# Expert products of a one-core decoder layer: only w3's second half stays an unsplit float32 product, and the down weights' parts move up in program order

## The chip, the cores and the metric

The kernel runs on one core of a Trainium2 chip. The metric is the device time of one execution in microseconds (us), median of the runs taken. The engines are named as the profile names them: PE (TensorE, the matmuls), PEld (its weight loads), ACT (ScalarE), DVE (VectorE), POOL (GpSimd) and SP (SyncE, which issues most transfers). Each engine runs its own instructions in order; they wait for one another on semaphores.

## The reference, cut to what matters

One layer of a decoder: stick-breaking attention and a state-space branch in parallel, then a mixture of experts with a final norm. The part that the change touches:

```python
def expert_block(args):
    xi, e = args                                   # 128 routed tokens, one of 32 experts
    hdn = jax.nn.silu(xi @ w1[e]) * (xi @ w3[e])   # 1024 -> 512
    return hdn @ w2[e]                             # 512 -> 1024
yb = lax.map(expert_block, (xb, block_e)).reshape(cap, d)
y = jax.ops.segment_sum(yb * slot_w[:, None], slot_tok, num_segments=t + 1)[:t]
```

All arrays are float32. There are 1024 tokens, 32 experts, and two experts for each token.

## The kernel before, in words

The program goes through the layer in stages; the experts are the last long one, the function `moe`. It loops over the 32 experts, one block of 128 token slots each. For expert e:

- `gather` (L1066) fetches the token rows by an indirect transfer, three experts ahead, into one of three row buffers.
- `xt` transposes the 128x1024 tokens on PE in two groups of four (L1088, into the PSUM tile `tr`). Tokens 0 to 511 of the model dimension are split: ACT copies them to float32r (`xh`), DVE subtracts that from the original (`xl`). The other half is copied by ACT as plain float32 (`xf`, L1090).
- The weights come as pages of 1 MB (128x2048 float32): w1 and w3 in two halves each, w2 in two halves, so six pages for each expert. SP loads them (L1052) into a ring of 14 page buffers named `r`, `m` and `x`, and waits for a buffer before each load.
- `unit` splits a page into two float32r tiles, the rounded part by ACT (L101) and the rest by DVE (L102). The two tiles are a pair; there are room and names for three pairs, `w` twice and `ms` once, given out in the order in which the program asks for units. A pair is taken over when the matmuls on its old unit are done.
- `up` multiplies. The first halves of w1 and w3 are units, with three matmuls for each 128 rows: high x high, high x low, low x high (L1112 to L1114). The second halves are unsplit float32 products with `xf` straight from the page (L1120). Both accumulate in the PSUM tiles `a1` and `a3`. Then ACT takes the sigmoid (L1126) and DVE multiplies twice (L1128), into the tile `mid`.
- `ht` transposes `mid` on PE (L1133) and splits the result into `hh` and `hl` (they are tile `w1_8641` in the rows below).
- `down` multiplies by the two units of w2, three matmuls for each 128x512 piece (L1145 to L1147), into `o0` and `o1`. ACT scales them into a row buffer (L1152) and POOL scatters it to DRAM (L1159).

In the loop, the down products of an expert run one expert late: the program order is `up(e)` first half, `ht` of e-1, `up(e)` second half, `xt(e+1)`, `down(e-1)`. The two w2 units are asked for inside `down`. A scheduler then sets the order of each engine's instructions; the tiles and their buffers keep the program's order. Each expert thus asks for four units: w1's and w3's first halves, then w2's two halves.

Of the kernel before, what the change touches and what calls it, by code (L numbers as in the profile page):

```python
# [12 lines left out]
F32 = mybir.dt.float32  # L13
F32R = mybir.dt.float32r
# [13 lines left out]
KD = D // 128  # L28
# [5 lines left out]
NE = 32  # L34
FF = 512
# [17 lines left out]
def _f(ap):  # L53
    return ap.bitcast(F32)
# [12 lines left out]
def drain(*gens):  # L67
    for g in gens:
        for _ in g:
            pass  # L70
# [924 lines left out]
def moe(tc, ctx, pool, i, ident, rt, ye_d, tab_d, h2_d, hg_d, split, con, out, rp, mp, wop, wop1, scale):  # L995
    nc = tc.nc
    V, A, P = nc.vector, nc.scalar, nc.gpsimd
    tab = rt["tab"]
    IO = bass.IndirectOffsetOnAxis
    XG, YB, NX, LAG = 3, 4, 2, 3  # L1000
# [5 lines left out]
    with ExitStack() as c:  # L1006
        ps = pool(c, "psb", space=PSUM)
        p = pool(c, "ex", bufs=2)

        rowr = [wop1.tile([128, 2, 512], F32R, name="w1", bufs=8) for _ in range(8)]  # L1010
        row = [_f(x).rearrange("p a b -> p (a b)") for x in rowr]
        hh, hl = (rowr[7][:, n].rearrange("p (a b) -> p a b", a=4) for n in range(2))
        xg, ss = row[:XG], p.tile([128, FF], F32, name="mid", bufs=1)
        ys = lambda e: row[XG + (e - NE + LAST) % YB]
        for x in xg:
            P.memset(x, 0.0)
# [4 lines left out]
        num = {}  # L1021
# [13 lines left out]
        raws, units = {}, {}  # L1035


        def view(t, shape):
            return t.rearrange("p a b -> p (a b)").rearrange("p (a b) -> p a b", a=shape[1])
# [5 lines left out]
        def ring(n, shape, r=False):  # L1045
            k = n if n < INIT else (n - INIT) % RING
            return page(*((rp, "r", 6) if k < 6 else (mp, "m", MR) if k < 12 else (p, "x", NX)), shape, r)

        def load(n):
            if n < len(src) and n not in raws:  # L1050
                raws[n] = ring(n, src[n][1])
                nc.sync.dma_start(raws[n], src[n][0])  # L1052

        def unit(n):

            if n not in units:
                load(n)
                pl, nm, b = (mp, "ms", 2) if len(units) % 3 == 2 else (wop, "w", 4)
                h, l = units[n] = [view(pl.tile([128, 4, FF], F32R, name=nm, bufs=b), src[n][1]) for _ in range(2)]
                split(h, l, raws[n], leng=P if n < HELD else V)  # L1060
            return units[n]

        def gather(e):
            if e >= NE - LAST:
                P.memset(xg[e % XG], 0.0)
            q = P.indirect_dma_start(out=xg[e % XG], out_offset=None, in_=hg_d, in_offset=IO(ap=tab[:, e, 0:1] if e else rt["idx"], axis=0),  # L1066
                                     bounds_check=S - 1, oob_is_err=False)
            first.append(q.ins)
# [11 lines left out]
        def xt(e):  # L1080

            x = xg[e % XG]
            xh, xl = (p.tile([128, 4, 128], F32R, name=n, bufs=1) for n in ("xh", "xl"))
            xf = p.tile([128, 4, 128], F32, name="xf", bufs=1)
            for q in range(2):
                tp = ps.tile([128, 4, 128], F32, name="tr", bufs=2)
                for k in range(4):
                    nc.tensor.transpose(tp[:, k], x[:, (q * 4 + k) * 128:(q * 4 + k) * 128 + 128], ident)  # L1088
                if q:
                    A.copy(xf, tp)  # L1090
                else:
                    parts[:] = split(xh, xl, tp)
            return xh, xl, xf

        gather(0)
        parts = []
        X = {0: xt(0)}
        read = rt["finish"](first[0], parts[1])
        with tc.issue_after(read):
# [6 lines left out]

        def up(e, xh, xl, xf):
            a = [ps.tile([128, 512], F32, name=n, bufs=2) for n in ("a1", "a3")]
            for w in range(2):
                h, l = unit(num[e, 0, w])  # L1110
                for k in range(4):
                    nc.tensor.matmul(a[w], lhsT=xh[:, k], rhs=h[:, k], start=(k == 0), stop=False)  # L1112
                    nc.tensor.matmul(a[w], lhsT=xh[:, k], rhs=l[:, k], start=False, stop=False)  # L1113
                    nc.tensor.matmul(a[w], lhsT=xl[:, k], rhs=h[:, k], start=False, stop=False)  # L1114
            yield
            for w in range(2):
                n = num[e, 1, w]
                load(n)
                for k in range(4):
                    nc.tensor.matmul(a[w], lhsT=xf[:, k], rhs=raws[n][:, k], start=False, stop=(k == 3))  # L1120
            yield

            s = ss.rearrange("p (k q) -> p k q", k=4)
            a = [x.rearrange("p (q k) -> p k q", k=4) for x in a]
            r = _f(tab[:, e, 3:4])
            A.activation(s, a[0], AF.Sigmoid, scale=r)  # L1126
            for n in range(2):
                V.scalar_tensor_tensor(s, a[n], r, s, op0=OP.mult, op1=OP.mult)  # L1128

        def ht():  # L1130
            tp = ps.tile([128, 4, 128], F32, name="tr", bufs=2)
            for k in range(4):
                nc.tensor.transpose(tp[:, k], ss[:, k * 128:k * 128 + 128], ident)  # L1133
            rooted[:] = split(hh, hl, tp)

        def down(e):
            o = [ps.tile([128, 512], F32, name=f"o{n}", bufs=1) for n in range(2)]
            for u in range(2):
                with tc.issue_after(rooted[0]) if e == NE - 1 and u else ExitStack():
                    h, l = unit(num[e, u, 2])  # L1140
                for n in range(2):
                    cs = slice(n * 512, n * 512 + 512)
                    for k in range(2):
                        kk = u * 2 + k
                        nc.tensor.matmul(o[n], lhsT=hh[:, kk], rhs=h[:, k, cs], start=(kk == 0), stop=False)  # L1145
                        nc.tensor.matmul(o[n], lhsT=hh[:, kk], rhs=l[:, k, cs], start=False, stop=False)  # L1146
                        q = nc.tensor.matmul(o[n], lhsT=hl[:, kk], rhs=h[:, k, cs], start=False, stop=(kk == 3))  # L1147
            done[:] = [q.ins]
            gate = _f(tab[:, e, 2:3])
            y = ys(e)  # L1150
            for n in range(2):
                A.activation(y[:, n * 512:n * 512 + 512], o[n], AF.Copy, scale=gate)  # L1152
            if e >= NE - LAST:
                yh, yl = last[e] = [wop1.tile([128, 2, 512], F32R, name="w1", bufs=8).rearrange("p a b -> p (a b)") for _ in range(2)]
                return lambda: split(yh, yl, y)
            scatter(e, y)
# [8 lines left out]
        def ahead(e):  # L1165
            for n in range(num[e, 0, 0], len(src)):
                load(n)

        def places():

            at = ring(len(src), [128, 2, D])
            P.iota(at[:, 0], pattern=[[1, S]], base=0, channel_multiplier=0, allow_small_or_imprecise_dtypes=True)
            hot = ring(len(src) + 1, [128, 2, S], True)
            for n in range(LAST):
                V.tensor_scalar(hot[:, n], at[:, 0], rt["tk"][:, NE - LAST + n:NE - LAST + n + 1], None, op0=OP.is_equal)
            g = at[:, 1]
            nc.sync.dma_start(g[:1], i["norm_final_g"].rearrange("(a d) -> a d", a=1))
            return hot, at

        def tiles(n, d, base):  # L1180

            b = []
            for t in range(0, NT, 2):
                b.append(ring(n + t // 2, [128, 2, D]))
                for k in range(2):
                    r = base + (t + k) * 128
                    nc.sync.dma_start(b[-1][:, k], d[r:r + 128, :])
            return b
# [7 lines left out]
        for e in range(NE):  # L1196
            g = up(e, *X[e])
            next(g)
            if e:
                ht()  # L1200
            if e == NE - 1:
                ahead(e)
                hot, at = places()
                res = tiles(len(src) + 2, h2_d, 0)
            drain(g)
            if e + XG < NE:
                gather(e + XG)
            if e + 1 < NE:
                X[e + 1] = xt(e + 1)
            if e:  # L1210
                parted = down(e - 1)
            if e == 1:
                zero = ys(3)
                P.memset(zero, 0.0)
                with tc.issue_after(first[-1]):
                    for n in range(NE - LAST, NE):
                        scatter(n, zero)
        overflow(at)
        ht()
        parted()  # L1220

        bs = []
        for t in range(0, NT, 2):
            n = len(src) + 6 + t
# [25 lines left out]
        for t in range(NT):  # L1250
            h, h1 = (x[:, t % 2] for x in bs[t // 2])
# [13 lines left out]
            ss, a, r, m = (p.tile([128, 1], F32, name=n) for n in ("ss", "ra", "rr", "rm"))  # L1265
# [136 lines left out]
```

## Time and profile before

| what | value |
|---|---|
| median of 3 runs | 1538.57 us (1536.74 to 1539.53) |
| the profiled execution | 1539.6 us, of which the span from first to last instruction is 1537.7 us |
| mean granted TensorE clock | 0.974 of full speed |
| PE busy | 1456.8 us, 95% of the span |
| DVE, ACT, POOL busy | 963.0, 722.3, 518.9 us |
| the expert stage | first token transposes at 864 us, last down product at 1493 us |

The profile is of one execution; its times are counted from the first instruction. Busy time is the time in which an instruction of the engine was running. A wait is the idle time of an engine before an instruction, put down to the instruction that released it.

### The profile page before, as it was taken

The page shows a single profiled execution, that of the slowest core. Times are in us where ns is not written, and L with a number is a line of the kernel's source. Part 1 is how long each engine was busy: PE and PEld are TensorE (multiplying, and loading weights), DVE is VectorE, ACT ScalarE, POOL GpSimd, SP SyncE. Part 2 cuts the span into 40 slices and gives each one's busy share as a digit, 9 for nine tenths or more (in the row PEclk, how much of TensorE's full clock was granted, in tenths as well). Part 3 has the DMA queues.
Part 4 walks back from the last instruction along what each step waited for, and adds up shares of the span by engine and source line. Part 5 has one row for each costly group of instructions (what it writes and reads, how often), then busy time and mean ns, then how long its engine had stood idle before and what let it go on. Part 6 is the DMA issues. An engine that isn't in the chain of part 4 may idle for free. (4 is left out here: it accounts for less than half of the span.)

```text
span 1537.7 us, 19509 instructions
## 1 busy us (share of the span) xinstructions
PE 1456.8 (95%) x6900; PEld 1123.4 (73%) x6900; DVE 963.0 (63%) x1488; ACT 722.3 (47%) x1141; POOL 518.9 (34%) x542
## 2 busy tenths in 40 slices
PE   7989799999999989999998799999999999999986
PEld 6967688998888867778787566666666666666663
DVE  6757565465756568665578566666665566656547
ACT  6212122455656577432223255555555455555543
POOL 1199941144444465332255321111111111111034
PEclk8999899999999999999999799999999999999998
DMA  8242344211111015264763799999999989999754
GB/s 256 77 104 72 92 104 97 60 42 54 30 51 34 28 44 142 78 198 160 268 247 124 286 346 356 352 354 353 356 360 351 353 342 358 334 334 357 271 200 163
DMA packets 132197, 314.77 MB, mean 205 GB/s; under 512 B 24305, under 2 KB 82289, under 8 KB 107522
## 3 DMA queue, kind: packets, MB, share of 16 engines
q1 hardware_dynamic: 120898, 295.99, 55.0%
q0 software_dynamic: 9728, 16.83, 2.9%
q8 instruction: 55, 0.90, 0.2%
q10 hardware_dynamic: 1472, 0.69, 0.2%
q14 instruction: 44, 0.36, 0.1%
HBM read 284.03 MB, written 44.11 MB: 213 GB/s over the span
## 5 line engine op out<-in xcount | busy, mean ns | idle before, releaser
L134 PE MATMUL mm<-xh,wh 128*128 128x512 f32 (+4 forms) x608 | 224.1, 369 | 1.1 <-DVE kl L691 0.6
L135 PE MATMUL mm<-xl,wh 128*128 128x512 f32 (+4 forms) x608 | 222.6, 366 | 0.0
L136 PE MATMUL mm<-xh,wl 128*128 128x512 f32 (+4 forms) x608 | 221.3, 364 | 0.8 <-DVE wl L102 0.8
L1159 POOL DMA_INDIRECT ye_d<-w,tab x32 | 56.1, 1754 | 250.0 <-ACT w L1152 249.4
L134 PEld LDWEIGHTS mm<-xh,wh 128*128 128x128 f32 x608 | 115.4, 190 | 16.0 <-issue 1.1
L136 PEld LDWEIGHTS mm<-xh,wl 128*128 128x128 f32 x608 | 115.4, 190 | 14.9 <-DVE wl L102 1.5
L135 PEld LDWEIGHTS mm<-xl,wh 128*128 128x128 f32 x608 | 115.3, 190 | 13.9 <-DVE xl L225 0.4
L754 DVE TENSOR_TENSOR_SCAN pr<-pr 128x144 f32<-128x144 f32 (+3 forms) x64 | 92.6, 1448 | 46.8 <-POOL pr L751 46.1
L102 DVE TENSOR_TENSOR w<-m,w 128x2048 fp32r<-128x2048 f32 x38 | 88.9, 2342 | 40.8 <-ACT w L101 40.7
L102 DVE TENSOR_TENSOR w<-r,w 128x2048 fp32r<-128x2048 f32 x36 | 82.2, 2291 | 47.6 <-ACT w L101 47.2
L1066 POOL DMA_INDIRECT w<-hg_d,tab x31 | 34.8, 1122 | 222.0 <-PE tr L1088 217.1
L755 POOL TENSOR_TENSOR be<-be,pr 128x143 f32<-128x143 f32 (+3 forms) x64 | 89.4, 1400 | 38.4 <-DVE pr L754 36.0
L1120 PE MATMUL a<-r,xf 128*128 128x512 f32 x224 | 100.7, 592 | 0.0
L1120 PE MATMUL a<-m,xf 128*128 128x512 f32 x208 | 93.3, 592 | 0.0
L1128 DVE SCALAR_TENSOR_TENSOR mid<-a,tab,mid 128x512 f32<-128x512 f32 x64 | 47.9, 749 | 63.8 <-ACT mid L1126 52.0
L101 ACT CAST w<-r 128x2048 fp32r<-128x2048 f32 x38 | 72.1, 1903 | 27.5 <-PE a L1113 14.4
L101 ACT CAST w<-m 128x2048 fp32r<-128x2048 f32 x38 | 72.5, 1907 | 18.9 <-PE o L1146 10.3
L101 ACT CAST wh<-wr 128x1024 fp32r<-128x1024 f32 (+1 forms) x44 | 44.6, 1014 | 65.8 <-PE mm L135 57.3
L1120 PEld LDWEIGHTS a<-r,xf 128*128 128x128 f32 x224 | 41.8, 190 | 42.3 <-issue 40.4
L102 DVE TENSOR_TENSOR wl<-wr,wh 128x1024 fp32r<-128x1024 f32 (+1 forms) x44 | 57.1, 1297 | 23.6 <-ACT wh L101 23.5
L1146 PE MATMUL o<-w,w 128*128 128x512 f32 x172 | 68.6, 399 | 3.2 <-DVE w L102 3.2
L751 POOL TENSOR_SCALAR_AFFINE_SELECT pr<-pr 128x128 f32<-128x128 f32 x64 | 26.3, 411 | 132.9 <-ACT pr L748 113.1
(534 smaller groups left out, 3766.2 us busy)
## 6 DMA issues: line engine op xcount, KB each, us to landing
r<-in_w_dram SPq DMA_DIRECT2D x84, 1024.0 KB, 7.9
m<-in_w_dram SPq DMA_DIRECT2D x82, 1024.0 KB, 8.1
x<-in_w_dram SPq DMA_DIRECT2D x26, 1024.0 KB, 7.9
wr<-in_w_in_dram SPq DMA_DIRECT2D x32, 512.0 KB, 4.2
gate_d<-gt SPq DMA_DIRECT2D x32, 256.0 KB, 2.3
x<-in_x_dram SPq DMA_DIRECT2D x8, 512.0 KB, 4.6
y<-y_d SPq DMA_DIRECT2D x16, 256.0 KB, 3.2
wr<-in_w_out_dram SPq DMA_DIRECT2D x8, 512.0 KB, 4.3
```

The source lines that it names most:

```text
L101: a = (A if heng is None else heng).copy(h, src)
L102: return a.ins, (V if leng is None else leng).tensor_sub(l, src, _f(h)).ins
L134: nc.tensor.matmul(ps, lhsT=wh, rhs=xh, start=first, stop=False)
L135: nc.tensor.matmul(ps, lhsT=wh, rhs=xl, start=False, stop=False)
L136: nc.tensor.matmul(ps, lhsT=wl, rhs=xh, start=False, stop=last)
L754: V.tensor_tensor_scan(rv, rv, rv, 1.0, op0=OP.mult, op1=OP.bypass)
L755: P.tensor_mul(be[:, :W - 1], be[:, :W - 1], pr[:, 1:W])
L1066: q = P.indirect_dma_start(out=xg[e % XG], out_offset=None, in_=hg_d, in_offset=IO(ap=tab[:, e, 0:1] if e else rt["idx"], axis=0), bounds_ ...
L1120: nc.tensor.matmul(a[w], lhsT=xf[:, k], rhs=raws[n][:, k], start=False, stop=(k == 3))
L1128: V.scalar_tensor_tensor(s, a[n], r, s, op0=OP.mult, op1=OP.mult)
L1146: nc.tensor.matmul(o[n], lhsT=hh[:, kk], rhs=l[:, k, cs], start=False, stop=False)
L1159: put = P.indirect_dma_start(out=ye_d, out_offset=IO(ap=tab[:, e, 1:2], axis=0), in_=y, in_offset=None, bounds_check=2 * S - 1, oob_is_err ...
```

## The change

The second half of w1 becomes a unit as well, so that each expert asks for five: w1 and w3 first halves, then (asked for right behind `ht` of e-1) the two halves of w2 for e-1, then w1's second half. Only w3's second half is left as an unsplit float32 product. `xh` and `xl` hold all 1024 rows, split in two groups, and stay one buffer each; `xf` is copied from the second group as before. The tile `mid` goes; its values stand in the expert's row buffer. L-numbers of the changed kernel: L1089 token transposes, L1119 to L1121 split products, L1114 float32 product, L1127 sigmoid, L1129 multiplications, L1134 transposes of `ht`, L1146 to L1148 down products, L1153 scaling. Three pairs of unit tiles and 14 page buffers are unchanged.

```diff
-        xg, ss = row[:XG], p.tile([128, FF], F32, name="mid", bufs=1)
+        xg = row[:XG]
...
-            xh, xl = (p.tile([128, 4, 128], F32R, name=n, bufs=1) for n in ("xh", "xl"))
+            xh, xl = (p.tile([128, KD, 128], F32R, name=n, bufs=1) for n in ("xh", "xl"))
...
-                if q:
-                    A.copy(xf, tp)
-                else:
-                    parts[:] = split(xh, xl, tp)
+                parts[:] = split(xh[:, q * 4:q * 4 + 4], xl[:, q * 4:q * 4 + 4], tp)
+            A.copy(xf, tp)
...
+            for u in range(2):
+                for w in range(2):
+                    n = num[e, u, w]
+                    if u and w:
+                        load(n)
+                        for k in range(4):
+                            nc.tensor.matmul(a[w], lhsT=xf[:, k], rhs=raws[n][:, k], start=False, stop=(k == 3))
+                        continue
+                    h, l = unit(n)
+                    for k in range(4):
+                        kk = u * 4 + k
+                        nc.tensor.matmul(a[w], lhsT=xh[:, kk], rhs=h[:, k], start=(kk == 0), stop=False)
+                        nc.tensor.matmul(a[w], lhsT=xh[:, kk], rhs=l[:, k], start=False, stop=False)
+                        nc.tensor.matmul(a[w], lhsT=xl[:, kk], rhs=h[:, k], start=False, stop=(kk == KD - 1))
+                yield
...
-            s = ss.rearrange("p (k q) -> p k q", k=4)
+            s = ys(e)[:, :FF].rearrange("p (k q) -> p k q", k=4)
...
+            if e:
+                for u in range(2):
+                    unit(num[e - 1, u, 2])
             drain(g)
```

How the change moves instructions. The numbers behind a name tell its tiles apart; of a pair, the lower is the rounded part and the next number the rest. First ACT, at the step from one expert to the next. Before, in the rows below, `xh_10281` are the tokens of the next expert, `w1_8639<-o0` and `o1` the scaling of a down product, and each cast of 128x2048 opens a unit:

```order
L1126 ACTIVATE mid_8642<-a1_10218,tab_8577 128x512
L101 CAST w_10344<-x_10342 128x2048
L101 CAST xh_10281<-tr_10284 128x512
L1090 COPY xf_10283<-tr_10291 128x512
L101 CAST w_10362<-x_10360 128x2048
L1152 ACTIVATE w1_8639<-o0_10297,tab_8577 128x512
L101 CAST ms_10423<-r_10421 128x2048
L1152 ACTIVATE w1_8639<-o1_10298,tab_8577 128x512
L101 CAST w_10441<-r_10439 128x2048
```

In the change, at the step from expert 13 (`a1_10401`) to expert 14 (`xh_10488`); `w_10559` is the first half of w3 and `ms_10541` the first half of w1 of expert 14, `w_10584` the first half of w2 of expert 13:

```order
L101 CAST w1_8641<-tr_10439 128x512
L101 CAST xh_10488<-tr_10491 128x512
L101 CAST w_10559<-x_10557 128x2048
L1127 ACTIVATE w1_8640<-a1_10401,tab_8577 128x512
L101 CAST xh_10488<-tr_10498 128x512
L101 CAST ms_10541<-x_10539 128x2048
L1153 ACTIVATE w1_8639<-o0_10506,tab_8577 128x512
L101 CAST w_10584<-r_10582 128x2048
L1153 ACTIVATE w1_8639<-o1_10507,tab_8577 128x512
L1091 COPY xf_10490<-tr_10498 128x512
L101 CAST w_10596<-r_10594 128x2048
```

There is one more cast of a page and one more of tokens in each expert, and the cast of the next expert's unit now stands in front of the sigmoid of the present one.

Second PE, at the step from expert 12 to 13 of the change. `o1_10371` is the last piece of the down product of expert 11 and `w_10318` the second half of its w2; `ms_10324` is the second half of w1 of expert 12; `w_10405` and `w_10423` are the first halves of w1 and w3 of expert 13:

```order
L1119 MATMUL a1_10265<-ms_10324,xh_10216 128x512
L1120 MATMUL a1_10265<-ms_10325,xh_10216 128x512
L1121 MATMUL a1_10265<-ms_10324,xl_10217 128x512
L1148 MATMUL o1_10371<-w_10318,w1_8641 128x512
L1119 MATMUL a1_10401<-w_10405,xh_10352 128x512
L1120 MATMUL a1_10401<-w_10406,xh_10352 128x512
L1119 MATMUL a3_10402<-w_10423,xh_10352 128x512
L1120 MATMUL a3_10402<-w_10424,xh_10352 128x512
L1121 MATMUL a1_10401<-w_10405,xl_10353 128x512
```

Before, the same step: `w_10563` is the second half of w2, `ms_10588` the first half of w1 of the next expert:

```order
L1146 MATMUL o1_10542<-w_10564,w1_8641 128x512
L1147 MATMUL o1_10542<-w_10563,w1_8641 128x512
L1112 MATMUL a1_10584<-ms_10588,xh_10525 128x512
L1113 MATMUL a1_10584<-ms_10589,xh_10525 128x512
L1114 MATMUL a1_10584<-ms_10588,xl_10526 128x512
```

The last down product's last matmul has come to stand behind the split product of w1's second half, and the next expert's first matmuls are mixed from its two units.

Third DVE, at the step from expert 14 to 15 of the change: `w_10678` and `ms_10696` are the rest parts of the first halves of w1 and w3 of expert 15, `w1_8637` the values of expert 14, `w_10721` the rest part of w2 for it:

```order
L102 TENSOR_TENSOR w_10678<-r_10675,w_10677 128x2048
L1129 SCALAR_TENSOR_TENSOR w1_8637<-a1_10537,tab_8577,w1_8637 128x512
L102 TENSOR_TENSOR xl_10625<-tr_10634,xh_10624 128x512
L102 TENSOR_TENSOR w_10721<-m_10718,w_10720 128x2048
L1129 SCALAR_TENSOR_TENSOR w1_8637<-a3_10538,tab_8577,w1_8637 128x512
L102 TENSOR_TENSOR ms_10696<-r_10693,ms_10695 128x2048
```

Before, the same step, with `w_10345`, `w_10363` and `ms_10424` the rest parts of three units:

```order
L1128 SCALAR_TENSOR_TENSOR mid_8642<-a1_10218,tab_8577,mid_8642 128x512
L102 TENSOR_TENSOR w_10345<-x_10342,w_10344 128x2048
L1128 SCALAR_TENSOR_TENSOR mid_8642<-a3_10219,tab_8577,mid_8642 128x512
L102 TENSOR_TENSOR xl_10282<-tr_10284,xh_10281 128x512
L102 TENSOR_TENSOR w_10363<-x_10360,w_10362 128x2048
L102 TENSOR_TENSOR ms_10424<-r_10421,ms_10423 128x2048
```

The two multiplications of an expert now have the next tokens' rest part and the subtraction for a w2 unit between them.

## Rows read from the trace of the kernel before

**Rows 1.** The page: busy times; granted clock in 40 slices of the span, in tenths.

```profile
PE 1456.8 (95%) x6900; PEld 1123.4 (73%) x6900; DVE 963.0 (63%) x1488; ACT 722.3 (47%) x1141; POOL 518.9 (34%) x542
...
PEclk8999899999999999999999799999999999999998
```

**Rows 2.** Windows: stretch, its us, PE, PEld, DVE, ACT, POOL busy, PEclk, DMA, GB/s.

```profile
1060.00:1120.00 60.00, 60.00 (x238) 41.22 (x237) 35.39 (x25) 34.74 (x31) 10.11 (x6) 1.00 0.94 351
```

**Rows 3.** Waits of PE over the whole span: total us, times, longest.

```profile
PE a L1261 <- DVEq L1291: 3.6, 1, 3.6
PE o L1146 <- DVE w L102: 3.2, 5, 1.2
```

**Rows 4.** Timeline of ACT: the sigmoids of experts 0 to 31 (six of 32).

```profile
874.76 0.69 ACT L1126 ACTIVATE mid<-a,tab 128x512 f32<-128x512 f32 x1 [1.76 <-PE a L1120]
...
888.95 0.69 ACT L1126 ACTIVATE mid<-a,tab 128x512 f32<-128x512 f32 x1 [1.76 <-PE a L1120]
...
905.57 0.69 ACT L1126 ACTIVATE mid<-a,tab 128x512 f32<-128x512 f32 x1 [1.96 <-PE a L1120]
...
1211.59 0.69 ACT L1126 ACTIVATE mid<-a,tab 128x512 f32<-128x512 f32 x1 [1.05 <-PE a L1120]
...
1308.40 0.69 ACT L1126 ACTIVATE mid<-a,tab 128x512 f32<-128x512 f32 x1 [4.51 <-PE a L1120]
...
1467.32 0.69 ACT L1126 ACTIVATE mid<-a,tab 128x512 f32<-128x512 f32 x1 [5.38 <-PE a L1120]
```

**Rows 5.** Timeline within one expert: float32 product, transposes, two low x high down matmuls.

```profile
1156.65 3.59 PE L1120 MATMUL a<-m,xf 128*128 128x512 f32 x8
...
1160.08 0.93 PE L1088 MATMUL tr<-ident,w 128*128 128x128 f32 x7
...
1161.31 0.39 PE L1147 MATMUL o<-w,w 128*128 128x512 f32 x1
...
1165.40 0.39 PE L1147 MATMUL o<-w,w 128*128 128x512 f32 x1
```

**Rows 6.** Groups of instructions, 1000 to 1400 us: busy us, mean ns; idle and releasers.

```profile
L102 DVE TENSOR_TENSOR w<-m,w 128x2048 fp32r<-128x2048 f32 x24 | 55.0, 2291 | 27.1 <-ACT w L101 26.9
L101 ACT CAST w<-m 128x2048 fp32r<-128x2048 f32 x24 | 45.8, 1907 | 11.9 <-PE o L1146 6.1 <-PE a L1113 5.6
L1128 DVE SCALAR_TENSOR_TENSOR mid<-a,tab,mid 128x512 f32<-128x512 f32 x42 | 31.4, 748 | 37.0 <-ACT mid L1126 31.0 <-PE a L1120 6.0
L102 DVE TENSOR_TENSOR xl<-tr,xh 128x512 fp32r<-128x512 f32 x21 | 14.4, 685 | 7.5 <-ACT xh L101 6.0 <-PE tr L1088 1.5
L101 ACT CAST xh<-tr 128x512 fp32r<-128x512 f32 x21 | 12.3, 586 | 37.1 <-PE tr L1088 27.7 <-PE a L1113 9.4
```

**Rows 7.** Waits and DMA, 900 to 1450 us: DVE's wait for a page, the weights' queue.

```profile
DVE w L102 <- DMA m<-in_w_dram: 0.4, 1, 0.4
...
q1 hardware_dynamic: 24081, 175.27, 85.0%
```

**Rows 8.** Timeline: a pair handed from PE to ACT to DVE; two DVE instructions without a gap.

```profile
1163.13 0.39 PE L1146 MATMUL o<-w,w 128*128 128x512 f32 x1
...
1163.56 1.91 ACT L101 CAST w<-m 128x2048 fp32r<-128x2048 f32 x1 [1.81 <-PE o L1146]
...
1165.50 2.29 DVE L102 TENSOR_TENSOR w<-m,w 128x2048 fp32r<-128x2048 f32 x1 [3.40 <-ACT w L101]
...
1218.80 2.28 DVE L102 TENSOR_TENSOR w<-x,w 128x2048 fp32r<-128x2048 f32 x1
1221.00 0.69 DVE L102 TENSOR_TENSOR xl<-tr,xh 128x512 fp32r<-128x512 f32 x1
```

**Rows 9.** PE after its 3.6 us wait: windows with PE busy, PEclk; its timeline.

```profile
1480.00:1483.00 3.00, 0.54 (x3) 0.97 0.03 5
1483.00:1486.00 3.00, 3.00 (x10) 0.50 0.87 294
...
1483.49 3.11 PE L1261 MATMUL a<-w,m 128*128 128x512 f32 x7
```

More of the change, by code (lines that the diff above doesn't have):

```diff
@@ L1108, in up @@
             a = [ps.tile([128, 512], F32, name=n, bufs=2) for n in ("a1", "a3")]
[L1109 to L1121, printed above, removed]
-            s = ss.rearrange("p (k q) -> p k q", k=4)
+            for u in range(2):
[14 more added lines that the diff above has]
+            s = ys(e)[:, :FF].rearrange("p (k q) -> p k q", k=4)
             a = [x.rearrange("p (q k) -> p k q", k=4) for x in a]
@@ L1128, in up, with ht @@
                 V.scalar_tensor_tensor(s, a[n], r, s, op0=OP.mult, op1=OP.mult)
-        def ht():
+        def ht(e):
             tp = ps.tile([128, 4, 128], F32, name="tr", bufs=2)
             for k in range(4):
-                nc.tensor.transpose(tp[:, k], ss[:, k * 128:k * 128 + 128], ident)
+                nc.tensor.transpose(tp[:, k], ys(e)[:, k * 128:k * 128 + 128], ident)
             rooted[:] = split(hh, hl, tp)
@@ L1199, in moe @@
             if e:
-                ht()
+                ht(e - 1)
             if e == NE - 1:
@@ L1218, in moe @@
         overflow(at)
-        ht()
+        ht(NE - 1)
         parted()
```

## Prediction

> **What bounds the kernel now.** I read the page first: PE is busy for 95% of the span [rows 1]. Then the windows of 60 us: in the expert stage PE is busy for all of each window at the full clock, while DVE and ACT have about 35 of 60 us and the DMA engines 0.94 [rows 2]. The waits of PE in the whole run add nearly nothing there: five waits for a subtraction, 3.2 us together [rows 3]. The timeline of the sigmoids gives the rhythm: from 905.57 to 1211.59 there are 16 steps, 19.13 us each [rows 4]. So PE's own work sets the step.
>
> That work can be priced from the timeline. Two low x high matmuls that have 18 matmuls between their starts lie 4.09 us apart, so a split matmul costs 0.227 us and a split product of four row groups (12 matmuls) 2.73 us. An unsplit float32 product is eight records, and from its start to the transposes that follow 3.43 us pass. Seven transposes took 0.93, so four cost about 0.44 with no tail [rows 5].
>
> Nothing else sets the pace before: DVE waited 0.4 us for a weight page in 550 us, and the weights' queue is busy for 85% [rows 7]. I take the pages as present after the change too; it adds no byte.
>
> **The change, part by part: PE.** Each expert loses one float32 product and gains one split product: 3.43 - 2.73 = 0.70 us less, so PE's step could be 18.43 us. The transposes stay as many. This is the whole possible gain: 32 x 0.70 = 22.5 us.
>
> **ACT and DVE.** Each expert gains a page's cast (1.91 us) and subtraction (2.29), a token cast (0.59) and subtraction (0.69) [rows 6]. DVE then has five subtractions of pages, three small ones and two multiplications: 5 x 2.29 + 3 x 0.69 + 2 x 0.75 = 15.0 us; ACT has less. Both fit into 18.4 us, so neither is the bound by its sum. `mid` gone and the sigmoid in the row buffer: ACT's sigmoid no longer waits for `ht`, which PE never waited for; it waits for the scatter of four experts before, which has some three steps of 19 us to land. I price it at nothing.
>
> **The three pairs.** This is what I think decides. A pair passes from one unit to the third one after it. Before, there were four units for each expert; the next expert's w1 took the pair of this expert's w3, done with long before the down products, and its cast and subtraction ran under the two float32 products. Now there are five: w1a, w3a, the two down units, w1b (a and b for the halves). The next w1a takes over the pair of the first down unit, the next w3a that of the second. Those are the last things that PE does in an expert. So the next w3a can't be cast before PE has finished its queue.
>
> What such a hand-over costs is in the timeline [rows 8]: a matmul started at 1163.13, ended 0.39 later, and the cast started 0.04 after that; it took 1.91, and with the subtraction of 2.29 a unit needs 4.2 us. Hand-overs cost about 0.03 each. An instruction right behind another starts some 0.1 before the printed end of the first (2.20 apart for a printed 2.28).
>
> **Played through.** I took the printed order of each engine and gave each instruction its start: the latest of its engine's being free, its inputs, and the last use of the old unit in its pair. The order repeats every three experts, with three kinds of step.
>
> At 12 to 13, PE stops after the last down matmul, which stands behind w1b. Count from there. The matmul's end and the hand-over come 0.20 later (0.39 + 0.04 - 0.23), when the cast of `w_10423` starts; in ACT's queue the tokens' cast stands behind it: 0.20 + 1.81 + 0.59 + 0.03 = 2.63 us of waiting. Three matmuls later (3.31) PE needs the rest part of `w_10423`: its subtraction starts at 2.14 and is ready at 2.14 + 2.29 + 0.03 = 4.46, a wait of 1.15. One matmul on (4.69) it needs `xl`, whose subtraction starts at 2.14 + 2.20 and is ready at 5.05: 0.36. Together 4.14.
>
> At 13 to 14, the cast of `w_10559` waits for the last down matmul: 0.20 + 1.91 + 0.03 = 2.14. One matmul runs, then the rest part is missing until 2.14 + 2.29 + 0.03 = 4.46: 2.09. Twelve matmuls on (7.19) PE needs the rest part of `ms_10541`. In DVE's queue, after the subtraction that began at 2.14, come a multiplication and `xl`, so this one starts at 2.14 + 2.20 + 0.65 + 0.59 = 5.58 and is ready at 7.90: 0.70. Together 4.93.
>
> At 14 to 15, `w_10677` takes the pair of the first down unit. Count from the start of its cast: its rest part is ready at 1.91 + 0.03 + 2.29 + 0.03 = 4.26, while PE has the second down unit and one matmul, until 2.75: 1.51. Eleven matmuls on (6.76) PE needs the cast of `ms_10695`; ahead of it in ACT's queue are this cast, the sigmoid, a token cast, `w_10720` and a scaling: 1.81 + 0.59 + 0.49 + 1.81 + 0.59 = 5.29, ready at 7.23: 0.46. One matmul on, the transposes of `ht` need the second multiplication. On DVE: 1.94 + 2.20 + 0.65 + 0.59 + 2.20 = 7.58, ready at 8.36, against 7.45: 0.89. After eight transposes (9.22), the down products need `hh`, behind that cast, a scaling, `xf` and one more cast: 5.29 + 1.81 + 0.59 + 0.49 + 1.81 = 9.99, ready at 10.59: 1.37. Together 4.23.
>
> Sum: 13.30 us of waits in three experts, or 4.43 each. Against 0.70 saved, the step grows by 3.73, from 19.13 to 22.86.
>
> If all 31 steps did so it would be +116 us. They don't. Going on in the same way: the first step is 23.1 us against 14.2 before; the next 22 together 494.5 against 419.5 (1308.40 - 888.95); the last eight 164.2 against 158.9, since the order is looser there; and from the last sigmoid to the last down product it is 9.2 us shorter. So 8.9 + 75.0 + 5.3 - 9.2 = +80. By the same play the order of before has a step of 19.06, 0.07 short of the trace [rows 4]; that shortfall over 31 steps adds 2, and the first sigmoid, one product later in the mixed start, 1: **+83**.
>
> **The clock.** In the trace, PE waited once for 3.6 us [rows 3]; after that the windows show a granted clock of 0.50, the lower of the two levels, for about 3 us, and seven matmuls took 3.11 us, 0.44 each instead of 0.23 [rows 9]: 1.5 us lost. The waits of at most 1.2 us in the expert stage left it at the highest digit, 9, in every slice from the 24th to the 38th [rows 1, 3]. The new waits lie between: 2.6, and 2.14 and 2.09 with one matmul between. There are about 15 such places. None falling gives 0, all falling 15 x 1.5 = 22 us. I take 5: most are nearer to 1.2 than to 3.6 as single waits. The Trainium skill ("TensorE: Matmul & The Clock Gate", "What's actually happening") says that the throttled state is the default and that only activity releases it. By that rule the pairs of waits with one matmul between would count as idle, and the sum would be nearer to the upper end; the fall after 3.6 us agrees with it, and no row here shows a wait of 2 to 3 us at full clock in this stage.
>
> **The sum.** The profiled execution took 1539.6 us (its span 1537.7), 1 us above the median of 1538.57. 1539.6 + 83 + 5 = 1627.6, or 1626.6 against the median; I say 1627. The unknowns: hand-overs from 0 to 0.08 us and back-to-back starts with or without the 0.1 overlap move the play between +80 and +108; the clock 0 to +22; and a real schedule can be kinder than my play by some 20.
>
> **Rivals.**
> - *PE stays the bound* (faster). If the next expert's pairs were ready when the down products end, the 0.70 would come through: 1538.6 - 22.5 = 1516. For it: PE is at 60 of 60 us now, and ACT and DVE sums fit. Against: the third-unit rule; it would need the waits of a step to stay under 0.70, and one subtraction alone (2.29) after a cast that can't start earlier exceeds that. Chance 0.05.
> - *Only the forced part waits.* By the pairs alone, with ACT's and DVE's queues always ready, a step loses just what 14 to 15 begins with: 1.51. Then 31 x (1.51 - 0.70) = 25: 1564. Against: the casts are in ACT's fixed order. Chance 0.05.
> - *The clock falls at each long wait.* 1538.6 + 83 + 22 = 1644, up to 1655 if all 21 steps of the pattern have it. For: 3.6 us did it. Chance 0.15.
> - *A tie* within 0.2% (3 us, about what a measurement of this kernel can tell from no change): waits would have to average 0.70 by accident. Chance 0.01.
>
> My forecast as priced has 0.74. The range from 1600 to 1655 takes in the play's bounds and most of the clock's rival; the first two rivals are left out. Faster 0.05, same 0.01, slower 0.94.
>
> **What would show it.** In the changed profile, the step between sigmoids (L1127) should repeat in threes of about 20.5, 28 and 20 us, 68 together instead of 57. PE should be busy for about 81% of the expert stage and have waits at L1119 and L1120 for `w` and `ms` from ACT and DVE, longest 2 to 3 us, some 100 us in all; ACT's casts should wait for the down products. PE's float32 records should halve. If PE is still at 60 of 60 us there and the step is 18.4, the third-unit argument is wrong; if PEclk falls below 1.00 in the stage, the clock's rival has a part.

## The result and the profile after

The changed kernel takes **1559.09 us** (median of 4 runs, 1555.82 to 1561.75), against 1538.51 for the kernel before on the same chip (4 runs, 1536.74 to 1539.53). The ratio is 1.0134, with a 95% interval of 1.0112 to 1.0156. So it is slower, by 20.6 us and not by the 88 of the forecast. The profiled execution took 1559.63 us, with a span of 1557.9.

The page of the changed kernel, its rows of busy time and of the granted clock, which answer to [rows 1]:

```profile
PE 1452.5 (93%) x7028; PEld 1149.6 (74%) x7028; DVE 1050.5 (67%) x1552; ACT 792.5 (51%) x1205; POOL 519.1 (33%) x542
...
PEclk8999899999999999999998999999999999999998
```

The window of [rows 2] in the changed kernel (the same columns):

```profile
1060.00:1120.00 60.00, 57.20 (x243) 42.30 (x244) 44.27 (x33) 40.22 (x39) 7.79 (x6) 1.00 0.95 347
```

PE no longer fills the window, but it lacks 3 us of 60, not the 19% that I expected. The longest waits of PE in the expert stage that the kernel before did not have (columns as in [rows 3]):

```profile
PE a L1120 <- DVE w L102: 8.3, 8, 1.2
PE o L1146 <- ACT w L101: 7.8, 10, 1.1
...
PE a L1119 <- ACT xh L101: 3.8, 11, 0.5
PE a L1120 <- DVE ms L102: 3.8, 5, 2.3
...
PE a L1119 <- ACT ms L101: 2.3, 2, 1.4
```

They are in the places that were named (the rest parts of units, from DVE, and casts, from ACT), but together 26 us, not 100. The sigmoids, which answer to [rows 4] (first, second, four in the middle, the 24th, the last):

```profile
876.25 0.68 ACT L1127 ACTIVATE w<-a,tab 128x512 f32<-128x512 f32 x1
895.11 0.69 ACT L1127 ACTIVATE w<-a,tab 128x512 f32<-128x512 f32 x1
...
1059.46 0.70 ACT L1127 ACTIVATE w<-a,tab 128x512 f32<-128x512 f32 x1
1074.15 0.69 ACT L1127 ACTIVATE w<-a,tab 128x512 f32<-128x512 f32 x1
1092.60 0.69 ACT L1127 ACTIVATE w<-a,tab 128x512 f32<-128x512 f32 x1
1118.76 0.70 ACT L1127 ACTIVATE w<-a,tab 128x512 f32<-128x512 f32 x1
...
1330.37 0.69 ACT L1127 ACTIVATE w<-a,tab 128x512 f32<-128x512 f32 x1
...
1499.37 0.69 ACT L1127 ACTIVATE w<-a,tab 128x512 f32<-128x512 f32 x1 [0.72 <-PE a L1121]
```

The rhythm does repeat in threes: 14.69, 18.45 and 26.16 us, 59.30 together. Before it was 57.4 (3 x 19.13).

**Where the time came from**, by these rows and [rows 4]. The first sigmoid comes 1.5 us later. The first step is 18.86 us against 14.19 (+4.7), the next 22 together 435.3 against 419.5 (+15.8), the last eight 169.0 against 158.9 (+10.1). From the last sigmoid to the start of the last down matmul it takes 12.4 us less (25.46 before, up to 1492.78; 13.06 in the change, up to 1512.43). Sum: +19.7, and the spans differ by 20.2.

Who hands a unit's buffers to whom stands in the groups of instructions of the changed kernel, 1000 to 1400 us (columns as in [rows 6]):

```profile
L101 ACT CAST w<-m 128x2048 fp32r<-128x2048 f32 x30 | 57.3, 1914 | 23.2 <-PE o L1147 14.7 <-PE a L1120 8.5
...
L102 DVE TENSOR_TENSOR w<-m,w 128x2048 fp32r<-128x2048 f32 x30 | 68.5, 2290 | 25.6 <-ACT w L101 22.4 <-PE o L1148 3.0
```

L1120 and L1147 are the high x low matmuls, the last to read a unit's rest part; L1121 and L1148 (low x high) are the last to read its rounded part. The casts wait for L1120 and L1147 only, and it is the subtractions that wait for L1148. So **the pair doesn't pass on as a pair**: the new rounded part goes into the old rest part's buffer, one matmul sooner, and the new rest part into the old rounded part's. The kernel before did the same: in [rows 6] and [rows 8] its casts wait for L1146, which is its high x low matmul. The description of the kernel, in which a pair is taken over as a whole, is wrong in this.

The timeline of the changed kernel around two hand-overs shows the other half:

```profile
1130.69 0.39 PE L1120 MATMUL a<-w,xh 128*128 128x512 f32 x1
...
1131.65 1.91 ACT L101 CAST w<-x 128x2048 fp32r<-128x2048 f32 x1
...
1136.85 0.39 PE L1148 MATMUL o<-w,w 128*128 128x512 f32 x1
...
1170.03 1.91 ACT L101 CAST w<-m 128x2048 fp32r<-128x2048 f32 x1 [3.82 <-PE o L1147]
...
1170.51 0.39 PE L1148 MATMUL o<-w,w 128*128 128x512 f32 x1
...
1172.98 1.92 ACT L101 CAST w<-m 128x2048 fp32r<-128x2048 f32 x1 [0.44 <-PE o L1147]
```

The cast at 1131.65 doesn't wait for the down products, which go on until 1137.2. The one at 1170.03 does wait for them, for L1147, and so does the next, at 1172.98; in this step the second half of w1 lies in `ms` (its matmuls start at 1170.74). Both kinds occur, and the pattern of three steps goes with their alternation.

### The profile page after: what moved, and what is told of

Its sections match the earlier page's. It is cut to its first block, busy times and chain, and to the rows that moved or that the text cites. A ratio compares the mean times of both kernels' runs of the same rounds, so it can differ in the third digit from the quotient of the medians.

```text
span 1557.9 us, 19965 instructions
## 1 busy us (share of the span) xinstructions
PE 1452.5 (93%) x7028; PEld 1149.6 (74%) x7028; DVE 1050.5 (67%) x1552; ACT 792.5 (51%) x1205; POOL 519.1 (33%) x542
## 5 line engine op out<-in xcount | busy, mean ns | idle before, releaser
L102 DVE TENSOR_TENSOR w<-m,w 128x2048 fp32r<-128x2048 f32 x46 | 105.9, 2311 | 40.7 <-ACT w L101 35.9
L102 DVE TENSOR_TENSOR w<-r,w 128x2048 fp32r<-128x2048 f32 x45 | 102.8, 2291 | 34.9 <-ACT w L101 31.6
L1120 PE MATMUL a<-w,xh 128*128 128x512 f32 x260 | 103.8, 399 | 8.8 <-DVE w L102 8.3
L1119 PE MATMUL a<-w,xh 128*128 128x512 f32 x260 | 107.1, 412 | 3.3 <-ACT xh L101 3.3
L101 ACT CAST w<-r 128x2048 fp32r<-128x2048 f32 x47 | 89.8, 1911 | 30.6 <-PE o L1147 14.9
L101 ACT CAST w<-m 128x2048 fp32r<-128x2048 f32 x46 | 87.9, 1914 | 33.5 <-PE o L1147 23.2
L1121 PE MATMUL a<-w,xl 128*128 128x512 f32 x260 | 102.3, 400 | 0.8
L102 DVE TENSOR_TENSOR xl<-tr,xh 128x512 fp32r<-128x512 f32 x64 | 42.8, 685 | 50.5 <-ACT xh L101 46.6
L1146 PE MATMUL o<-w,w 128*128 128x512 f32 x168 | 66.3, 401 | 7.0 <-ACT w L101 7.0
L101 ACT CAST xh<-tr 128x512 fp32r<-128x512 f32 x64 | 36.3, 588 | 70.1 <-PE a L1120 61.9
```

What stands on the lines that cost most here:

```text
L101: a = (A if heng is None else heng).copy(h, src)
L102: return a.ins, (V if leng is None else leng).tensor_sub(l, src, _f(h)).ins
L1119: nc.tensor.matmul(a[w], lhsT=xh[:, kk], rhs=h[:, k], start=(kk == 0), stop=False)
L1120: nc.tensor.matmul(a[w], lhsT=xh[:, kk], rhs=l[:, k], start=False, stop=False)
L1121: nc.tensor.matmul(a[w], lhsT=xl[:, kk], rhs=h[:, k], start=False, stop=(kk == KD - 1))
```

## The experiments

Three theories went into the first four runs. Their names stand in the expectations; in short, A is that the buffers pass on in the order in which their old units are done with, and that the early request for the down units' buffers is what makes this dear. The kernel before had a median of 1540.68 us (17 runs) beside the first four and 1540.8 (15 runs) beside the last three.

### The change without the early request

```diff
-            if e:
-                for u in range(2):
-                    unit(num[e - 1, u, 2])
```

The down units are asked for inside `down` again, as before; w1's second half stays a unit.

> The change without its last part: the w2 units are asked for inside the down products again, five units for each expert stay. Theory A (a pair's two buffers pass on one by one in the order in which their old units are done with, not to the third unit after): the next w1's cast then finds a buffer early, and the order printed for this kernel, played with the durations of the rows, has steps of 18.4 us from expert 2 to about 13 and some 20 us in the later ones; the total comes out within 5 us of before, about 1540. Theory B (the change is slow because ACT and DVE carry a fifth unit): as slow as the change, about 1559, with steps of 19.8 on average from the start. Theory C (third-unit rule, as in the prediction): waits of 1.5 us or more in every step, above 1560.

Measured: **1543.93 us** (9 runs), ratio 1.0025 [1.0011, 1.0039]. A window of 60 us, the casts of 1000 to 1400 us, and two sigmoids that have ten steps between them:

```profile
1000.00:1060.00 60.00, 60.00 (x265) 45.84 (x264) 44.84 (x32) 41.85 (x39) 6.35 (x7) 1.00 0.97 367
...
L101 ACT CAST w<-m 128x2048 fp32r<-128x2048 f32 x30 | 57.3, 1917 | 2.3 <-PE a L1120 2.2
...
931.14 0.69 ACT L1127 ACTIVATE w<-a,tab 128x512 f32<-128x512 f32 x1
...
1115.61 0.70 ACT L1127 ACTIVATE w<-a,tab 128x512 f32<-128x512 f32 x1
```

The casts' wait for the down products is all but gone (in this group 14.7 us in the change and none here; in the group from `r` 13.9 and 0.6), PE fills the window again, and the ten steps take 18.45 us each. That is the step of 18.43 that the prediction worked out for a PE that sets the pace. In the whole the gain doesn't show: the second step is 22.85 us, and the last 16 steps (1150.70 to 1475.76) average 20.3. So a fifth unit asked for late costs about 4 us in all, and 17 of the change's 20.6 us (1.0134 against 1.0025) hang on the early request.

### The early request alone, in the kernel before

```diff
+            if e:
+                for u in range(2):
+                    unit(num[e - 1, u, 2])
```

> The kernel before with only the early request of the w2 units; four units for each expert and two float32 products as before. Theory A: the four units have slack, so the steps stay at 19.1 us up to expert 18 and the total rises by some 4 us, to about 1543, in the later experts alone. Theory B: no fifth unit, so no change at all, 1538.5. If the early request were the whole loss of the change by itself, it would be about 1559.

Measured: **1544.61 us** (9 runs), ratio 1.0034 [1.0019, 1.0049]. The same window:

```profile
1000.00:1060.00 60.00, 60.00 (x238) 41.08 (x237) 37.71 (x27) 33.82 (x31) 10.11 (x6) 1.00 0.94 347
```

With four units for each expert the early request leaves PE at 60 of 60 us and the step at 19.12, up to the sigmoid at 1212.09; the loss is in the later steps, as A had it. So each half of the change costs 4 to 5 us alone; the two together cost 20.

### The third-unit rule, made true

The prediction's rule, written into the changed kernel: the six buffers become three fixed pairs, and each unit takes the pair of the third one before it.

```diff
+        w4 = [wop.tile([128, 4, FF], F32R, name="w", bufs=4) for _ in range(4)]
+        pairs = [w4[:2], w4[2:], [mp.tile([128, 4, FF], F32R, name="ms", bufs=2) for _ in range(2)]]
...
-                h, l = units[n] = [view(pl.tile([128, 4, FF], F32R, name=nm, bufs=b), src[n][1]) for _ in range(2)]
+                h, l = units[n] = [view(x, src[n][1]) for x in pairs[len(units) % 3]]
```

> The change with its six unit buffers held as three fixed pairs, each unit taking the pair of the third unit before it, the rounded part always in the same buffer: the rule that the prediction took for granted. Theory A: this is a different kernel from the change; the order printed for it, played with the durations of the rows, alternates between steps of 26.6 and 14.1 us, 40.7 for two experts, and comes out 33 us above before, about 1571, 10 above the change. Theory C (that this is what the change does already): the same time as the change, 1559, and its pattern of 14.7, 18.5 and 26.2 us.

Measured: **1575.82 us** (4 runs), ratio 1.0239 [1.0214, 1.0264]. The casts (1000 to 1400 us), PE's two longest groups of waits, and three sigmoids:

```profile
L101 ACT CAST w<-m 128x2048 fp32r<-128x2048 f32 x27 | 51.5, 1906 | 26.4 <-PE a L1122 14.9 <-PE o L1149 11.5
...
PE a L1121 <- DVE w L102: 23.2, 21, 1.4
PE a L1121 <- DVE ms L102: 12.3, 10, 2.3
...
1000.48 0.72 ACT L1128 ACTIVATE w<-a,tab 128x512 f32<-128x512 f32 x1
1014.91 0.69 ACT L1128 ACTIVATE w<-a,tab 128x512 f32<-128x512 f32 x1
1041.54 0.71 ACT L1128 ACTIVATE w<-a,tab 128x512 f32<-128x512 f32 x1
```

Lines stand one lower here, so L1122 and L1149 are the low x high matmuls: now the casts wait for a pair's last use, as the rule wants. The rhythm is another (14.43 and 26.63 by these rows, in twos instead of threes), and PE waits longer. So the changed kernel doesn't follow the rule; following it costs 16 us more (1.0239 against 1.0134). It doesn't cost the +83 that I added up either, but 35 (1575.82 against 1540.68): for fixed pairs the scheduler made another order, one that repeats every two experts and not every three.

### Everything split

From the changed kernel: w3's second half becomes a unit too, the float32 product and its copy of the tokens go, and the down units are asked for late.

```diff
-            A.copy(xf, tp)
...
-                    if u and w:
+                    if False:
...
-            if e:
-                for u in range(2):
-                    unit(num[e - 1, u, 2])
```

> No unsplit product left: w3's second half is a unit too, six for each expert, and the w2 units are asked for inside the down products. Theory A: PE's step falls by another 0.7 us to 17.7; the printed order, played, has steps of 17.7 up to expert 11 and 18.9 later, and the total is about 1518. Theory B: a sixth unit makes it slower than the change, above 1570. DVE's work is 17.2 us in each expert, so it can't be much faster than that.

Measured: **1521.41 us** (4 runs), ratio 0.9881 [0.9862, 0.9900]. It beats both kernels. Two windows:

```profile
1000.00:1060.00 60.00, 60.00 (x287) 49.94 (x287) 56.62 (x40) 50.17 (x43) 13.60 (x7) 1.00 0.99 382
1060.00:1120.00 60.00, 56.32 (x262) 45.59 (x261) 49.63 (x35) 43.66 (x38) 10.98 (x7) 1.00 0.94 350
```

Up to about the tenth step PE fills the window at 17.72 us for a step, another 0.73 below 18.45: the second float32 product is worth what the first was. DVE has 56.6 of 60 us there. Afterwards most steps are 19 to 20.

### A fourth pair for the change

Runs one and two left a question: does the early request hurt through the buffers, or through the place of its casts in ACT's queue? Here the changed kernel keeps its requests and has eight unit buffers; two page buffers go for them (the pages for the stage behind the experts use the new buffers too).

```diff
-    XG, YB, NX, LAG = 3, 4, 2, 3
+    XG, YB, NX, LAG = 3, 4, 0, 3
...
+            if n >= len(src) + 12 and len(src) == 6 * NE:
+                return page(p, "q", 2, shape, r)
...
-                pl, nm, b = (mp, "ms", 2) if len(units) % 3 == 2 else (wop, "w", 4)
+                pl, nm, b = ((wop, "w", 4), (wop, "w", 4), (mp, "ms", 2), (p, "q", 2) if len(units) < 156 else (wop, "w", 4))[len(units) % 4]
```

> The changed kernel with eight unit buffers instead of six (a fourth pair), made out of two page buffers fewer; the order in which units are asked for is that of the change. A (the early request is dear because the next w3a then gets buffers that are still being read): with a fourth pair the waits of the three kinds of step go, the first ten steps are about 18.4 us each, as without the early request, and the whole is 4 us above before, 1543 (1538 to 1550). B (the early request is dear by the place of its casts in ACT's queue alone, whatever the buffers): the pattern 14.7, 18.5, 26.2 stays, about 1559. C (two pages fewer starve DVE): new waits for pages, over 1559.

Measured: **1536.15 us** (6 runs), ratio 0.9969 [0.9957, 0.9982], against 1.0134 for the change, some 25 us less. Its window, two sigmoids that have seven steps between them, and its casts (900 to 1084 us):

```profile
1000.00:1060.00 60.00, 60.00 (x263) 45.81 (x263) 44.97 (x33) 40.56 (x40) 8.08 (x7) 1.00 0.96 368
...
894.01 0.69 ACT L1129 ACTIVATE w<-a,tab 128x512 f32<-128x512 f32 x1
...
1023.13 0.69 ACT L1129 ACTIVATE w<-a,tab 128x512 f32<-128x512 f32 x1
...
L101 ACT CAST w<-m 128x2048 fp32r<-128x2048 f32 x12 | 23.0, 1918 | 1.4 <-PE a L1122 1.3
```

The pattern of three is gone, each of the seven steps takes 18.45 us, and the casts hardly wait for the down products (not at all in this group, 0.6 us in the one from `r` to `ms`). So the early request is not dear whatever the buffers (B), and there is no want of pages (C): it takes the six buffers (A). The time came out 7 us below what A expected, and below its range. The scheduler's order is another one here too: in these seven steps ACT's order is that of the change's 18.45 us step (1074.15 to 1092.60), and the orders of its other two steps do not occur. The run doesn't part the wait for a buffer from the order that was made for six buffers.

### The same fourth pair in the kernel before, and with everything split

The controls: eight unit buffers and two page buffers fewer, by the same edit, in the kernel before and in the version with all units split.

> The kernel before with the same eight unit buffers and two page buffers fewer: the control for the run with the fourth pair. A: TensorE sets its step already, so the steps stay at 19.1 us and the time within 4 us of before. C (two pages fewer cost by themselves): over 1545.

> All six units of an expert split (no float32 product, no copy of the tokens for one), no early request, eight unit buffers and two page buffers fewer. A: TensorE's own work for a step is 17.7 us here, and the version with six buffers came to 1521; by replaying the orders the fourth pair does not help further: 1521 within 5. B (buffers still bound that version's later steps of 19 us): with a fourth pair these fall too, 1500 or less.

Measured: **1540.17 us** (10 runs), ratio 1.0002 [0.9987, 1.0017], and **1522.5 us** (4 runs), ratio 0.9872 [0.9855, 0.9889]. A window of the first, then one of the second and its longest waits of PE:

```profile
1000.00:1060.00 60.00, 60.00 (x239) 41.10 (x238) 38.05 (x26) 35.71 (x32) 10.11 (x6) 1.00 0.93 352
```

```profile
1060.00:1120.00 60.00, 56.30 (x266) 45.77 (x266) 49.01 (x35) 43.34 (x36) 9.29 (x7) 1.00 0.94 340
...
PE a L1121 <- DVE q L102: 10.4, 10, 1.1
PE a L1121 <- DVE w L102: 10.3, 10, 1.1
```

The fourth pair does nothing for the time of the kernel before, whose steps were PE's own already, and nothing for the fully split version. The two pages fewer do show in the kernel before: DVE waited for pages 4.5 us between 900 and 1450 us, against 0.4 [rows 7], without a cost in the time. So its 25 us in the change belong to the early request with five units. The later steps of about 19 us in the split version stay with a fourth pair, so B of that run falls: six buffers aren't what holds them up. What PE waits for there is the rest part of a unit, about 1.05 us at a time.

## Why the prediction was wrong

**What bounds the kernel: right.** With a fourth pair and without the early request, PE fills its windows and the step is 18.45 us. I had 18.43, from 0.70 saved for each product. The steps show 19.13 - 18.45 = 0.68, and the fully split version 0.73 for the next product.

**Pages, ACT and DVE: right.** DVE had no wait for a page in the changed kernel's expert stage, and neither DVE nor ACT was the bound by its sum (44.27 and 40.22 of 60 us). The sigmoid in the row buffer, priced at nothing, cost nothing: the only idle time of ACT in front of the 32 sigmoids is the 0.72 us of the last.

**The step that failed is "A pair passes from one unit to the third one after it", and with it "The next w1a takes over the pair of the first down unit, the next w3a that of the second."** I read the three pairs as a ring. Two things are different, and the rows of before already showed one of them:

- Buffers of one name go on in the order in which their old units are done with in the program; this is read from the releasers of the casts, and theory A's times for the first four runs, worked out on it beforehand, came within 5 us of the measured ones. w1's second half asks last, but in program order its matmuls stand before the down products, so its pair comes free before theirs. Where it lies in `w`, which it does in two experts of three, the next w1a or w3a gets its pair and need not wait for the end of PE's queue. Only in the third expert, where it lies in `ms`, do both take over the down units' pairs: that is the cast at 1170.03, and the long step around it.
- Within a pair the new rounded part takes the rest part's buffer, so its cast starts one matmul sooner. [Rows 8] had this: the cast there waits for L1146, not for the low x high matmul behind it. I took its duration from that row and didn't ask which matmul it waited for.

Played through again with this in place of the ring, and nothing else altered, the same printed order gives steps of 14.41, 18.35 and 26.17 us, 58.93 together (an estimate of mine, from the durations in the rows, and made after the result). The trace has 59.30. So three steps lose 59.30 - 3 x 18.45 = 3.95 us, where my three sums (4.14, 4.93, 4.23) had 13.30. In a step that is 1.32 lost against 0.68 saved, so the sign was right and the size was not: 22 steps grew by 15.8 us instead of 75.0. That is 59 of the 68 us by which the time was missed; the first step (+4.7, not +8.9) and the tail (-12.4, not -9.2) make 7 more, while the last eight steps cost 5 more than I had. The 6 or so that are left are the +3 for the play's shortfall and the start, of which 1.5 came, and the clock's +5, which the measured steps hold already.

The run with fixed pairs shows that even the rule, where it is true, isn't worth what I made of it. I combined an order that the scheduler had made for one way of handing on with another way, and an order goes with its own buffers.

**The clock: the size right by luck, the places in part.** I took 5 us. In the changed kernel's stage it fell three times, at 999, 1296 and 1460 us. By the sigmoids the step of 14.69 us is 16.32 where it fell (998.52 to 1014.84 and 1295.60 to 1311.92), 1.63 each, and the third time it lasted about twice as long: some 6 us. The third followed two waits with one matmul between, the kind that I had in mind; the first two followed a single stop of 1.2 us, which I had not counted on (last section).

**The rivals.** "Only the forced part waits" gave 1564, close to the time, but not by its mechanism: it holds the ring and takes the queues as ready. With the ring made true the time is 1575.82. "PE stays the bound" is what the fourth pair gives for its first seven steps, but not for the whole: 1536, not 1516. "The clock falls at each long wait" didn't happen: it fell at three places.

**What stays open.** In every version but the one with fixed pairs the steady steps end before the stage does. The kernel before is no exception: its last 13 steps in [rows 4], from 1211.59 to 1467.32, take 19.7 us each, where it had 19.13. With five units asked for late, with five and a fourth pair, and with everything split it comes sooner, after some eight to fifteen experts, and the later steps average 19 to 20 us although PE's own work stays the same. That is where 1516 was lost: with the fourth pair the eight steps up to 1023.13 took 147.1 us and the 23 after them 453.7, 19.7 each. In these versions DVE waited for no page between 900 and 1450 us, and for the split version more unit buffers don't help.

What the traces do show is that the engines' order is another one from there on. In the fully split version with a fourth pair ACT has the cast of a page (1010.33) between the two scalings of a down product (1009.41 and 1012.14), in each step between the sigmoids at 896.47 and 1039.05, and in only two after that. In most of the later steps the scalings come one behind the other, and the casts after them:

```profile
1255.37 0.69 ACT L1154 ACTIVATE w<-o,tab 128x512 f32<-128x512 f32 x1 [0.45 <-PE o L1149]
...
1256.43 1.92 ACT L101 CAST w<-r 128x2048 fp32r<-128x2048 f32 x1
...
1260.72 0.50 PE L1121 MATMUL a<-w,xh 128*128 128x512 f32 x1 [1.06 <-DVE w L102]
```

The cast at 1256.43 had no wait of its own; it stood in ACT's queue behind a scaling that waited for the down product. The rest part that goes with it was ready at 1260.66, and it is what PE waited 1.06 us for. With fixed pairs the order and the two steps repeat up to the last expert (26.59 and 14.15 us). The orders that were printed, played before the runs, also had the later steps (18.4 and then some 20 for the change without the early request, 17.7 and then 18.9 for everything split). So I put the later steps down to the scheduler's order, but that is argued: no run held the order fixed, and why the order changes is open.

## What to carry to other kernels

When a change makes something ask for its buffers earlier, find out who hands a buffer to whom before any wait is priced: the timeline shows it, in the instruction named as the releaser of the first one to write the buffer, and it need be neither the oldest request nor the same tile of the pair. An earlier request for buffers holds them for longer; check whether the next units, whose data are wanted sooner, then get those that are read last. A gain for the engine that sets the pace counts only as long as the buffers keep up, and one more pair, paid for with two page buffers whose loss cost no time here, turned this change from 20.6 us slower to 4.7 us faster than the kernel before.

## What the runs showed of the hardware

Two stretches of PE's timeline in the changed kernel, the same instructions one pattern of three steps apart, up to the same stop:

```profile
998.56 0.50 PE L1120 MATMUL a<-w,xh 128*128 128x512 f32 x1 [1.20 <-DVE w L102]
999.16 0.65 PE L1121 MATMUL a<-w,xl 128*128 128x512 f32 x1
999.60 0.63 PE L1119 MATMUL a<-w,xh 128*128 128x512 f32 x1
...
1059.50 0.49 PE L1120 MATMUL a<-w,xh 128*128 128x512 f32 x1 [1.19 <-DVE w L102]
1060.10 0.50 PE L1121 MATMUL a<-w,xl 128*128 128x512 f32 x1
1060.44 0.40 PE L1119 MATMUL a<-w,xh 128*128 128x512 f32 x1
1060.67 0.39 PE L1120 MATMUL a<-w,xh 128*128 128x512 f32 x1
```

A window right behind the first, and the third place, near the end of the stage:

```profile
999.50:1001.00 1.50, 1.50 (x5) 1.12 (x5) 1.50 (x2) 0.83 (x2) 0.92 (x1) 0.50 0.94 251
```

```profile
1458.47 0.50 PE L1119 MATMUL a<-ms,xh 128*128 128x512 f32 x1 [1.38 <-ACT ms L101]
1461.29 0.80 PE L1120 MATMUL a<-ms,xh 128*128 128x512 f32 x1 [2.31 <-DVE ms L102]
1461.88 0.63 PE L1121 MATMUL a<-ms,xl 128*128 128x512 f32 x1
```

After the stop of 1.20 us at 998.56 the granted clock is at 0.50, the lower of its two levels, and matmuls start 0.43 us apart instead of 0.23; after the one of 1.19 us before 1059.50 they are 0.23 apart again from the third on. Two waits with one matmul between, 1.38 and 2.31, were followed by the lower level too (0.50 from 1462 to 1466), as the prediction's pairs of waits would have been by its upper end. I had not expected that a stop so short could be followed by a fall at all (in [rows 3] waits of 1.2 left the clock alone), nor that two equal stops would end differently. Of the steps of this kind that follow the pattern, four show 14.67 to 14.69 us and two 16.32. Nor did a longer stop have to bring it: 3.04 us without a matmul at the end of the stage were followed by a granted clock of 1.00 (from 1502.36 to 1504.50), and six matmuls took 1.66 us, where seven had taken 3.11 after the 3.6 us of the kernel before [rows 9].

```profile
1502.36 1.66 PE L1266 MATMUL a<-w,m 128*128 128x512 f32 x6 [3.04 <-DVEq L1296]
```
